# Swapping the halves of the S5 state with copies on ScalarE, and S5 chunk kernels in column quarters

## The chip, the cores and the metric

One core of a Trainium2 chip runs the whole program. The metric is the time of one execution in microseconds (us) on the device; everything is fp32 at the borders. The engines are named as in the profile: PE is TensorE (PEld its weight loads), DVE is VectorE, ACT is ScalarE, POOL is GpSimd, and SP is SyncE, which issues the DMAs.

## The reference

Two blocks run one after the other on 512 tokens of width 1024. The second block (two layers of convolution, neighbourhood attention and feed-forward) isn't touched. The first block mixes the tokens, behind 16 meta tokens, with two state-space branches, SSD and S5, and an MLP follows. The change lies in the S5 branch:

```
bu_re = einsum('blgh,gph->blgp', u, bb_re)      # bb = coef * b, 64 groups g of 16 features h, 64 states p
bu_im = einsum('blgh,gph->blgp', u, bb_im)
# associative scan over the tokens l of s[l] = a * s[l-1] + bu[l], a complex, |a| = exp(lr * step)
_, _, s_re, s_im = lax.associative_scan(combine, (a_re, a_im, bu_re, bu_im), axis=1)
y = einsum('blgp,ghp->blgh', s_re, c_re) - einsum('blgp,ghp->blgh', s_im, c_im) + u * d_skip
y = gelu(y, approximate=False)
v = y @ w_glu + b_glu
y = v[..., :D_S5] * sigmoid(v[..., D_S5:])
```

## The kernel before

**The stages.** `in_proj` makes S5's input u in a layout of chunks of 8 tokens (66 chunks, so 528 columns for the 8 groups of a feature tile). Then the string `ORDER` names the steps of the S5 stage one by one: `P` is `s5_prepare(m)` (the matrices of feature tile m, m from 0 to 7), `S` is `s5_scan(m)`, `x` and `z` are tiles of the input projections for the SSD branch (`xbc_proj`, `z_proj`), `d` and `e` belong to the SSD decays and `r` is `s5_result` (gelu and a split in two parts of one tile). Behind it come `glu`, mixed with the SSD chunks, and the rest. The scans lie between 70 and 276.6 us of the execution.

**Preparing a tile.** `s5_prepare(m)` builds, for the 8 groups of a tile, X (L804 to L806; turned by the `XT` transposes into P, L812), Y (L825), and the kernel within a chunk: eight products `Kp` of 16 rows (L833), four into each of two PSUM tiles, which ACT copies to K (L835, 16x512). DVE adds the skip term to K, and eight DMAs lay it out as the block matrix M (L846).

**Scanning a tile.** The states of the chunks lie with their real parts on partitions 0 to 63 and their imaginary ones on 64 to 127. `s5_scan(m)` makes tables of cosines `cs` and sines `sn` of the chunks' rotations (`sincos`, L781 to L784), makes the chunk states with 2x4 products `S` (L870) and copies each half to SBUF on ACT (L872). To rotate them, each half is multiplied by the constant matrix `perm`, which swaps the two sets of partitions and turns the sign of one (`Sp`, L874); DVE multiplies the result by `sn` (L875), S by `cs` (L876), and adds (L877). Then `tensor_tensor_scan` runs the recurrence over the chunks with the magnitudes `mag8` (L879 copies them to f, L882 is the scan), and the result Z is rotated back in the same way with two more products with `perm` (`Zp`, L885 to L888). Sixteen products `y` (L891 with M, L893 with the states) give the output, which ACT copies to `ye` (L896); SP writes it to DRAM (`yD`, L897). `s5_result` reads it back as `yt` (L903), and ACT makes gelu (L905) and the high part `y5..h` (L909), which `glu` multiplies by its weights.

**Weights.** `W` (L234 to L242) loads a block of weights (`raw`, on SP), ACT casts its high part `whi` (L240) and DVE subtracts it from the block to get the low part `wlo` (L242). `mm3` (L248 to L250) makes three products of each pair of tiles. There are two buffers for `raw` and three for each of the parts.

**What sets the order.** Each engine runs its instructions in one order, which the tile framework's scheduler makes at build time from the program order and from priorities: loads and splits of weights come ahead (`high_priority`), and PE's products of the steps `x` and `z` are laid between the products of a scan. There is one queue for each engine; an instruction that waits holds back all behind it. PSUM has four tiles for the projections (`gps`) and four for all else (`mps`); small tables lie in pools of 16 (`s2`) and 8 (`b4`) buffers.

The matrix, from `constants`:

```
for m in range(64):
    c[m + 64, 256 + m] = 1.0
    c[m, 256 + 64 + m] = -1.0
```

## Time and profile before

| | |
|---|---|
| runs | 2776.68, 2771.53, 2775.11 us; median 2775.11 |
| span of the profiled execution | 2775.2 us (no time around the span is shown for it) |
| PE busy | 2717.2 us, 98% |
| DVE busy | 2020.9 us, 73% |
| ACT busy | 1161.1 us, 42% |
| mean granted clock of TensorE | 0.994 |

The span runs from the first instruction to the last. A share is an average over stages with different limits; the rows of the section on the trace are from the S5 stage and from what follows it directly. In rows of the timeline and of groups, "x2" is a number of records: a float32 product of PE leaves two records, and its start to the next start is the time that it takes in the stream. A bracket at the end of a row tells how long the engine was idle before it and what ended that.

### The profile page before, as it was taken

How to read it: one execution, taken by the hardware profiler on the slowest of the kernel's cores; microseconds unless marked ns; L12 is line 12 of the kernel's file. 1: busy time of each engine (PE TensorE's matmuls, PEld its weight loads, DVE VectorE, ACT ScalarE, POOL GpSimd, SP SyncE). 2: the span in 40 equal slices, each digit the busy share in tenths (PEclk: the TensorE clock that was granted, in tenths of full speed). 3: DMA queues.
4: the chain of work that ended last, by engine and by line, in shares of the span. 5: the costliest groups of instructions: out<-in, count | busy, mean ns of one | idle time of the engine just before them, and what ended most of it. 6: DMA issues, size and time to landing. Idle time of an engine off the chain costs nothing.

```text
span 2775.2 us, 40532 instructions
## 1 busy us (share of the span) xinstructions
PE 2717.2 (98%) x15512; PEld 2340.6 (84%) x15512; DVE 2020.9 (73%) x3969; ACT 1161.1 (42%) x1945; POOL 6.0 (0%) x52
## 2 busy tenths in 40 slices
PE   8999899999999999999999999999999999999998
PEld 8888678788988998878888888888887888988887
DVE  7987678898875575897669888644759966655546
ACT  4443653433444453444454232323553453533333
POOL 0000000000000000000000000000000000000000
PEclk9999999999999999999999999999999999999999
DMA  6223444465432345222324446221342223232332
GB/s 213 68 78 90 115 134 161 159 202 186 132 110 86 121 142 177 95 77 83 101 93 135 155 144 220 96 61 61 105 142 88 86 67 88 91 99 90 103 97 76
DMA packets 157394, 321.08 MB, mean 116 GB/s; under 512 B 39760, under 2 KB 60688, under 8 KB 157200
## 3 DMA queue, kind: packets, MB, share of 16 engines
q1 hardware_dynamic: 157200, 318.49, 36.6%
q8 instruction: 122, 2.00, 0.3%
q14 instruction: 72, 0.59, 0.1%
HBM read 306.53 MB, written 9.54 MB: 114 GB/s over the span
## 4 chain that ended last, share of the span: by engine, by line
PE 80%; DVE 11%; DMA 4%; ACT 3%; issue 2%; SPq 0%; DVEq 0%; ACTq 0%; POOL 0%
PE lat1fu L248 3%; PE lat1fu L249 3%; PE lat1fu L250 3%; DVE wlo L242 3%; PE lat0fu L249 3%; PE lat0fu L248 3%; PE lat0fu L250 3%; PE up L248 2%; PE up L249 2%; PE up L250 2%; PE dn L248 2%; PE dn L249 2%; PE dn L250 2%; PE lat0d L249 1%; PE lat0d L250 1%
## 5 line engine op out<-in xcount | busy, mean ns | idle before, releaser
L240 ACT CAST whi<-raw 128x1024 fp32r<-128x1024 f32 (+3 forms) x486 | 456.8, 940 | 864.7 <-PE ctx0d L249 113.8
L242 DVE TENSOR_TENSOR wlo<-raw,whi 128x1024 fp32r<-128x1024 f32 (+3 forms) x486 | 527.2, 1085 | 204.0 <-ACT whi L240 199.3
L249 PE MATMUL ctx0fu<-ctx0fx,whi 128*128 128x256 f32 x352 | 99.7, 283 | 0.0
L250 PE MATMUL ctx0fu<-ctx0fx,wlo 128*128 128x256 f32 x352 | 99.6, 283 | 0.0
L248 PE MATMUL ctx0fu<-ctx0fx,whi 128*128 128x256 f32 x352 | 99.5, 283 | 0.0
L1134 DVE SCALAR_TENSOR_TENSOR lat1cv<-lat1u,vect,lat1cv 128x512 f32<-128x512 f32 x120 | 86.2, 750 | 0.6
L1134 DVE SCALAR_TENSOR_TENSOR lat0cv<-lat0u,vect,lat0cv 128x512 f32<-128x512 f32 x120 | 86.1, 746 | 0.6
L1453 DVE SCALAR_TENSOR_TENSOR lat0fc<-lat0fu,vect,lat0fc 128x511 f32<-128x511 f32 x44 | 32.9, 749 | 62.7 <-ACT lat0fc L1452 62.7
L248 PEld LDWEIGHTS ctx0fu<-ctx0fx,whi 128*128 128x128 f32 x352 | 67.4, 191 | 1.6
L249 PEld LDWEIGHTS ctx0fu<-ctx0fx,whi 128*128 128x128 f32 x352 | 67.4, 191 | 1.6
L250 PEld LDWEIGHTS ctx0fu<-ctx0fx,wlo 128*128 128x128 f32 x352 | 67.4, 191 | 0.0
L1452 ACT ACTIVATE lat0fc<-lat0fu,vect 128x512 f32<-128x512 f32 x44 | 34.2, 778 | 74.1 <-PE lat0fu L250 74.1
L1493 DVE SCALAR_TENSOR_TENSOR hT<-lat1d,mod1lat,hT 128x512 f32<-128x512 f32 (+1 forms) x40 | 25.5, 644 | 48.2 <-PE lat1d L250 48.0
L1134 DVE SCALAR_TENSOR_TENSOR cxcv<-cxu,vect,cxcv 128x256 f32<-128x256 f32 x120 | 52.3, 485 | 0.7
L250 PE MATMUL ctx0d<-ctx0fh,wlo 128*128 128x256 f32 x176 | 49.9, 285 | 0.3 <-DVE wlo L242 0.3
L248 PE MATMUL ctx0d<-ctx0fh,whi 128*128 128x256 f32 x176 | 49.5, 282 | 0.4 <-ACT whi L240 0.4
L249 PE MATMUL ctx0d<-ctx0fh,whi 128*128 128x256 f32 x176 | 49.8, 284 | 0.0
L985 DVE TENSOR_TENSOR hT<-hT,dn 128x512 f32<-128x512 f32 x40 | 27.5, 687 | 23.1 <-PE dn L250 23.1
L978 DVE SCALAR_TENSOR_TENSOR r<-up,rsbm 128x512 f32<-128x512 f32 x32 | 22.1, 691 | 30.2 <-PE up L250 29.9
L1493 DVE SCALAR_TENSOR_TENSOR hT<-lat0d,mod0lat,hT 128x512 f32<-128x512 f32 x32 | 23.9, 748 | 20.7 <-PE lat0d L250 20.6
L250 PE MATMUL cxg<-cxn1x,wlo 128*128 128x256 f32 x128 | 37.4, 292 | 0.6 <-DVE wlo L242 0.6
L249 PE MATMUL cxg<-cxn1x,whi 128*128 128x256 f32 x128 | 37.5, 293 | 0.0
(3025 smaller groups left out, 9140.4 us busy)
## 6 DMA issues: line engine op xcount, KB each, us to landing
raw<-in_p_in SPq DMA_DIRECT2D x100, 512.0 KB, 3.7
aw<-in_ada SPq DMA_DIRECT2D x192, 256.0 KB, 3.1
raw<-in_p_up SPq DMA_DIRECT2D x88, 512.0 KB, 3.7
raw<-in_p_dn SPq DMA_DIRECT2D x48, 384.0 KB, 3.1
raw<-in_w_up SPq DMA_DIRECT2D x32, 512.0 KB, 3.7
raw<-in_p_cn SPq DMA_DIRECT2D x48, 256.0 KB, 2.6
raw<-in_w_down SPq DMA_DIRECT2D x24, 384.0 KB, 3.0
raw<-in_p_out SPq DMA_DIRECT2D x18, 512.0 KB, 3.8
```

The lines of the kernel that those rows point to most:

```text
L240: nc.scalar.copy(hi, raw)
L242: nc.vector.tensor_sub(lo, raw, hi.bitcast(F32))
L248: mm(ps, w[0], x[0], start=first, stop=False)
L249: mm(ps, w[0], x[1], start=False, stop=False)
L250: mm(ps, w[1], x[0], start=False, stop=last)
L978: V.scalar_tensor_tensor(r, ps, 0.0, rsb, op0=ALU.max, op1=ALU.mult)
L985: V.tensor_add(h[f], h[f], ps)
L1134: V.scalar_tensor_tensor(ac, u[:, k:k + n], self.vec(f"cdw{l}", 4 * k + i), ac, op0=ALU.mult, op1=ALU.add)
L1452: A.activation(u, ps[:, :n], AF.Identity, scale=wv(1), bias=self.vec(f"fdwb{l}", t))
L1453: V.scalar_tensor_tensor(u[:, 1:], ps[:, :n - 1], wv(0), u[:, 1:], op0=ALU.mult, op1=ALU.add)
L1493: V.scalar_tensor_tensor(x, ps, self.mod[l, kind][:, 40 + f:41 + f], x, op0=ALU.mult, op1=ALU.add)
```

## The change

In `s5_scan` the four products with `perm` go, and with them the matrix. ACT copies the chunk states out of PSUM in four pieces of 64 partitions, each to the other half (S then holds the swapped states), and DVE takes the states that aren't swapped from PSUM (`R = ps * cs`). The sign is put into the sine: `sincos` gets a scale for each partition, `turn` = -2 pi sgn. After the scan ACT copies Z in two pieces of 64x528 to the other half, into f, and DVE makes two products of 528 columns where it made four of 264. In `s5_prepare` the four `Kp` products of a half go to PSUM partitions 0, 32, 64 and 96 of one tile (so to four quarters of the array's columns), the halves side by side; ACT copies each quarter with both halves, four copies of 16x2x128. The constants shrink from 588 columns to 460. Removed comments shift the lines.

```diff
@@ -75,9 +75,9 @@
 ROWV = {"dt_bias": (0, 16), "a_log": (16, 16), "d_ssd": (32, 16), "log_step": (48, 64),
         "lam_re": (112, 64), "lam_im": (176, 64)}
 NROW = 240
-CST = {"ident": (0, 128), "tri": (128, 128), "perm": (256, 128), "ones": (384, 128),
-       "cidx": (512, 66), "sgn": (578, 1), "kidx": (579, 9)}
-NCST = 588
+CST = {"ident": (0, 128), "tri": (128, 128), "ones": (256, 128),
+       "cidx": (384, 66), "sgn": (450, 1), "kidx": (451, 9)}
+NCST = 460
 
 
 def constants():
...
@@ -725,6 +722,8 @@
         t = self.b4("pt", 576).rearrange("p (g k) -> p g k", k=9)
         V.tensor_tensor(f, r.unsqueeze(2).to_broadcast([P, 64, 9]),
                         self.C("kidx").unsqueeze(1).to_broadcast([P, 64, 9]), op=ALU.mult)
+        self.turn = self.bp.tile([P, 1], F32, name="turn")
+        V.tensor_scalar(self.turn, self.C("sgn"), -TWO_PI, None, op0=ALU.mult)
         self.r8 = self.bp.tile([P, 64], F32, name="r8")
         self.mag8 = self.bp.tile([P, 64], F32, name="mag8")
         A.copy(self.mag8.unsqueeze(2), pm[:, :, 8:9])
...
@@ -773,18 +772,19 @@
         for t in self.M5:
             nc.gpsimd.memset(t, 0.0)
 
-    def sincos(self, f, t, sn, cs):
+    def sincos(self, f, t, sn, cs, scale=TWO_PI):
         V, A = self.nc.vector, self.nc.scalar
         V.tensor_scalar(t, f, MAGIC, MAGIC, op0=ALU.add, op1=ALU.subtract)
         V.tensor_sub(f, f, t)
         A.activation(cs, f, AF.Sin, scale=TWO_PI / 2)
-        A.activation(sn, f, AF.Sin, scale=TWO_PI)
+        A.activation(sn, f, AF.Sin, scale=scale)
         A.activation(cs, cs, AF.Square)
         V.tensor_scalar(cs, cs, -2.0, 1.0, op0=ALU.mult, op1=ALU.add)
 
     def s5_prepare(self, m):
         nc = self.nc
         V, A, T = nc.vector, nc.scalar, nc.tensor
         gs = slice(8 * m, 8 * m + 8)
...
@@ -824,15 +824,17 @@
             V.tensor_tensor(y4(Y2), g4(self.Gi), c4(C2), op=ALU.mult)
             V.tensor_sub(Yq, Yq, Y2)
         Yg = Y.rearrange("p (g n) -> p g n", g=8)
         Kt = self.b4(f"K{m}", 1024).rearrange("p (g n) -> p g n", g=8)
+        ps = self.mps(f"Kp{m}")
         for q in range(2):
-            ps = self.mps(f"Kp{m}_{q}")
             for r in range(4):
                 g = 4 * q + r
-                T.matmul(ps[:16, r * P:(r + 1) * P], B1[:, g * 16:(g + 1) * 16], Yg[:, g, 0:P],
-                         start=True, stop=True)
-            A.copy(Kt[:16, 4 * q:4 * q + 4].rearrange("p g n -> p (g n)"), ps[:16])
+                T.matmul(ps[32 * r:32 * r + 16, q * P:(q + 1) * P], B1[:, g * 16:(g + 1) * 16],
+                         Yg[:, g, 0:P], start=True, stop=True)
+        Kq = Kt.rearrange("p (q r) n -> p r q n", r=4)
+        for r in range(4):
+            A.copy(Kq[:16, r], ps[32 * r:32 * r + 16, :2 * P].rearrange("p (q n) -> p q n", q=2))
         dI = self.s2(f"dI{m}", P)[:16]
         with self.tc.high_priority(offset=100):
             nc.sync.dma_start(dI, self.I["d5"][:, m * P:(m + 1) * P])
...
@@ -847,21 +849,22 @@
         return Pm, Yg, M
 
     def s5_scan(self, m, mats):
         nc = self.nc
         V, A, T = nc.vector, nc.scalar, nc.tensor
         gs = slice(8 * m, 8 * m + 8)
         Pm, Yg, M = mats
         f, t = self.s2(f"f{m}"), self.s2(f"t{m}")
         sn, cs = self.s2(f"sn{m}"), self.s2(f"cs{m}")
         v3 = lambda x: x.rearrange("p (g c) -> p g c", c=NCH)
         V.tensor_tensor(v3(f), self.r8[:, gs].unsqueeze(2).to_broadcast([P, 8, NCH]),
                         self.C("cidx").unsqueeze(1).to_broadcast([P, 8, NCH]), op=ALU.mult)
-        self.sincos(f, t, sn, cs)
+        self.sincos(f, t, sn, cs, self.turn)
         U = self.hT[S5U[m]]
         S, R = self.s2(f"S{m}"), t
+        halves = ((slice(0, 64), slice(64, P)), (slice(64, P), slice(0, 64)))
         hf = [slice(0, HALF), slice(HALF, TOK)]
         for q in range(2):
             ps = self.mps(f"S{m}_{q}")
...
@@ -869,22 +872,20 @@
                 g = 4 * q + r
                 T.matmul(ps[:, r * NCH:(r + 1) * NCH], Pm[:, g * P:(g + 1) * P],
                          U[:, g * NCH:(g + 1) * NCH], start=True, stop=True)
-            A.copy(S[:, hf[q]], ps[:, :HALF])
-            pp = self.mps(f"Sp{m}_{q}")
-            T.matmul(pp[:, :HALF], self.C("perm"), S[:, hf[q]], start=True, stop=True)
-            V.tensor_mul(f[:, hf[q]], pp[:, :HALF], sn[:, hf[q]])
-            V.tensor_mul(R[:, hf[q]], S[:, hf[q]], cs[:, hf[q]])
+            for a, b in halves:
+                A.copy(S[a, hf[q]], ps[b, :HALF])
+            V.tensor_mul(R[:, hf[q]], ps[:, :HALF], cs[:, hf[q]])
+            V.tensor_mul(f[:, hf[q]], S[:, hf[q]], sn[:, hf[q]])
         V.tensor_add(R, R, f)
         m8 = f
         A.copy(v3(m8), self.mag8[:, gs].unsqueeze(2).to_broadcast([P, 8, NCH]))
         nc.gpsimd.memset(v3(m8)[:, :, 0:1], 0.0)
         Z = S
         V.tensor_tensor_scan(Z, m8, R, 0.0, op0=ALU.mult, op1=ALU.add)
-        for q in range(2):
-            pp = self.mps(f"Zp{m}_{q}")
-            T.matmul(pp[:, :HALF], self.C("perm"), Z[:, hf[q]], start=True, stop=True)
-            V.tensor_mul(f[:, hf[q]], pp[:, :HALF], sn[:, hf[q]])
-            V.tensor_mul(R[:, hf[q]], Z[:, hf[q]], cs[:, hf[q]])
+        for a, b in halves:
+            A.copy(f[a], Z[b])
+        V.tensor_mul(R, Z, cs)
+        V.tensor_mul(f, f, sn)
         V.tensor_sub(R, R, f)
         py = self.mps(f"y5{m}")
         for g in range(8):
```

Where this moves instructions is read from the order in which each engine's instructions stand. PE at the scan of tile 2 before: the second K group (`Kp`), the state products with a `perm` product behind each half (`S`, `Sp`), the swap of the scan's result (`Zp`), and the first `y`; the `xbc` rows are the filler.

```order
L249 MATMUL xbc_0_2205<-xg0l,whi_2201 128x264
L833 MATMUL Kp_1_1435<-Y_1419,bc_1395 16x128 x4
L870 MATMUL S_0_1465<-hT_85,P_1151 128x66 x4
L250 MATMUL xbc_0_2139<-xg0h,wlo_2137 128x264
L250 MATMUL xbc_1_2140<-xg0h,wlo_2137 128x264
...
L249 MATMUL xbc_0_2139<-xg2l,whi_2135 128x264
L874 MATMUL Sp_0_1471<-S_1464,cst 128x264
L870 MATMUL S_1_1475<-hT_85,P_1151 128x66 x4
...
L885 MATMUL Zp_0_1489<-S_1464,cst 128x264
L885 MATMUL Zp_1_1493<-S_1464,cst 128x264
L891 MATMUL y_1498<-hT_85,M_0_640 128x64
L250 MATMUL xbc_0_2139<-xg7h,wlo_2137 128x264
```

PE at the same place after: the K groups lie around both halves of S, and what follows the second one is 74 `xbc` products and then the `y` products.

```order
L833 MATMUL Kp_1422<-Y_1412,bc_1388 16x128 x4
L873 MATMUL S_0_1459<-hT_85,P_1149 128x66 x4
L873 MATMUL S_1_1468<-hT_85,P_1149 128x66 x4
L892 MATMUL y_1486<-hT_85,M_0_642 128x64
...
L833 MATMUL Kp_1422<-Y_1412,bc_1388 16x128 x4
L247 MATMUL xbc_0_2112<-xg0h,wlo_2110 128x264
...
L245 MATMUL xbc_0_2178<-xg5h,whi_2174 128x264
L246 MATMUL xbc_0_2178<-xg5l,whi_2174 128x264
L894 MATMUL y_1486<-t_1448,Y_1162 128x64
L892 MATMUL y_1486<-hT_85,M_0_642 128x64
```

Both halves' `Sp` and the two `Zp` are gone, the first `y` has moved ahead of the second K group, and no product that waits for the scan stands between the K group and the second `y`.

ACT at the same scan before: the copies of K, the tables, the copies of S, a weight cast, the magnitudes.

```order
L835 COPY K_1428<-Kp_0_1429 16x512
L835 COPY K_1428<-Kp_1_1435 16x512
L781 ACTIVATE cs_1456<-f_1453 128x528
L782 ACTIVATE sn_1455<-f_1453 128x528
L783 ACTIVATE cs_1456<-cs_1456 128x528
L872 COPY S_1464<-S_0_1465 128x264
L872 COPY S_1464<-S_1_1475 128x264
L240 CAST whi_2390<-raw_2388 128x1024
L879 COPY f_1453<-mag_578 128x528
```

And after, with the two copies of Z at the end:

```order
L837 COPY K_1421<-Kp_1422 16x2x128 x4
L781 ACTIVATE cs_1450<-f_1447 128x528
L782 ACTIVATE sn_1449<-f_1447,turn 128x528
L783 ACTIVATE cs_1450<-cs_1450 128x528
L876 COPY S_1458<-S_0_1459 64x264 x2
L876 COPY S_1458<-S_1_1468 64x264 x2
L237 CAST whi_2358<-raw_2356 128x1024
L881 COPY f_1447<-mag_580 128x528
L886 COPY f_1447<-S_1458 64x528 x2
```

The order of the kinds is kept; the K copies, now all four behind both K groups, stand ahead of the cosine as before, and two copies of Z have come in behind the magnitudes.

ACT at the end of the stretch (tile 7) before, up to the copy of the output; the four `z` are activations of the last z tiles:

```order
L872 COPY S_2711<-S_0_2712 128x264
L872 COPY S_2711<-S_1_2722 128x264
L240 CAST whi_3262<-raw_3260 128x1024
L879 COPY f_2700<-mag_578 128x528
L240 CAST whi_3295<-raw_3293 128x1024
L589 ACTIVATE z_2779<-z_0_3068,rs1k 128x256
L589 ACTIVATE z_2780<-z_0_3068,rs1k 128x256
L589 ACTIVATE z_2781<-z_1_3069,rs1k 128x256
L589 ACTIVATE z_2782<-z_1_3069,rs1k 128x256
L240 CAST whi_3445<-raw_3443 128x1024
L896 COPY ye_2762<-y_2745 128x512
```

And after:

```order
L876 COPY S_2679<-S_0_2680 64x264 x2
L876 COPY S_2679<-S_1_2689 64x264 x2
L586 ACTIVATE z_2741<-z_0_3030,rs1k 128x256
L586 ACTIVATE z_2742<-z_0_3030,rs1k 128x256
L237 CAST whi_3224<-raw_3222 128x1024
L881 COPY f_2668<-mag_580 128x528
L586 ACTIVATE z_2743<-z_1_3031,rs1k 128x256
L586 ACTIVATE z_2744<-z_1_3031,rs1k 128x256
L237 CAST whi_3257<-raw_3255 128x1024
L886 COPY f_2668<-S_2679 64x528 x2
L237 CAST whi_3407<-raw_3405 128x1024
L897 COPY ye_2724<-y_2707 128x512
```

Two `z` activations now stand ahead of the copy of the magnitudes, and all four and two weight casts ahead of the copies of Z.

SP at the end of the stretch before, where `raw` are glu's weights:

```order
L234 DMA raw_3260<-in_w_glu 128x1024
L234 DMA raw_3293<-in_w_glu 128x1024
L695 DMA hT_86<-in_xT 128x512
L234 DMA raw_3443<-in_w_glu 128x1024
L234 DMA raw_3476<-in_w_glu 128x1024
L695 DMA hT_88<-in_xT 128x512
L897 DMA yD_210<-ye_2762 128x512
L903 DMA yt_2765<-yD_203 128x8x64
```

And after:

```order
L231 DMA raw_3222<-in_w_glu 128x1024
L231 DMA raw_3255<-in_w_glu 128x1024
L692 DMA hT_86<-in_xT 128x512
L231 DMA raw_3405<-in_w_glu 128x1024
L231 DMA raw_3438<-in_w_glu 128x1024
L231 DMA raw_3472<-in_w_glu 128x1024
L904 DMA yt_2727<-yD_203 128x8x64
L898 DMA yD_210<-ye_2724 128x512
```

A further `raw` load has come ahead of the write of tile 7's output, the one `hT` load has moved behind, and the first `yt` load has passed the write of `yD`.

## Rows read from the trace of the kernel before

**Rows 1.** The page, part 1: busy us (share of the span) xinstructions.
```profile
PE 2717.2 (98%) x15512; PEld 2340.6 (84%) x15512; DVE 2020.9 (73%) x3969; ACT 1161.1 (42%) x1945; POOL 6.0 (0%) x52
```

**Rows 2.** Windows: stretch, length, busy PE PEld DVE ACT POOL (records), clock, DMA share, GB/s.
```profile
70.00:276.60 206.60, 198.20 (x1556) 184.13 (x1554) 176.04 (x303) 85.01 (x144) 1.91 (x18) 1.00 0.28 78
```

**Rows 3.** PE's waits to 300 us: us in total, times, longest us.
```profile
PE glug L248 <- ACT y50h L909: 8.0, 1, 8.0
...
PE Zp L885 <- DVE S L882: 3.6, 8, 0.7
...
PE xbc L248 <- ACT whi L240: 2.3, 3, 1.5
...
PE Sp L874 <- ACT S L872: 0.6, 3, 0.2
```

**Rows 4.** Lines: ns min/median/max, first and last start us, forms.
```profile
L872 ACT COPY S<-S x16: 349/375/382, 89.6 to 269.0; 128x264 f32<-128x264 f32 x16
...
L782 ACT ACTIVATE sn<-f x8: 627/628/639, 88.0 to 264.8; 128x528 f32<-128x528 f32 x8
...
L879 ACT COPY f<-mag x8: 632/633/640, 94.9 to 271.4; 128x528 f32<-128x528 f32 x8
```

**Rows 5.** Timeline of the scan of tile 2: start us, us, engine line op.
```profile
146.13 0.28 PE L250 MATMUL xbc<-xg2h,wlo 128*128 128x264 f32 x1
...
146.35 0.71 PE L874 MATMUL Sp<-S,cst 128*128 128x264 f32 x2
...
147.02 0.28 PE L249 MATMUL xbc<-xg3l,whi 128*128 128x264 f32 x1
...
148.20 1.22 DVE L242 TENSOR_TENSOR wlo<-raw,whi 128x1024 fp32r<-128x1024 f32 x1
...
149.33 1.25 DVE L882 TENSOR_TENSOR_SCAN S<-f,t 128x528 f32<-128x528 f32 x1
...
149.95 0.28 PE L249 MATMUL xbc<-xg7l,whi 128*128 128x264 f32 x1
...
150.73 1.13 PE L885 MATMUL Zp<-S,cst 128*128 128x264 f32 x4 [0.50 <-DVE S L882]
...
151.69 0.33 PE L891 MATMUL y<-hT,M 128*128 128x64 f32 x2
...
152.59 0.70 DVE L888 TENSOR_TENSOR t<-t,f 128x528 f32<-128x528 f32 x1
```

**Rows 6.** Chain that ended last, 105 to 170 us: start us, us, what.
```profile
165.30 1.85 PE Kp L833 x16
```

**Rows 7.** Timeline of the end of the stretch: start us, us, engine line op.
```profile
276.61 0.84 ACT L589 ACTIVATE z<-z,rs1k 128x256 f32<-128x256 f32 x2 [2.90 <-PE z L250]
...
276.89 0.43 PE L893 MATMUL y<-t,Y 128*128 128x64 f32 x2 [0.32 <-DVE t L888]
...
281.10 1.28 ACT L905 ACT_TABLE_LOAD   x1
...
281.47 8.79 SPq L903 DMA_DIRECT2D yt<-yD  x8
...
286.05 0.63 ACT L905 ACTIVATE yt<-yt 128x512 f32<-128x512 f32 x1 [3.67 <-DMA yt<-yD]
...
288.80 0.80 PE L248 MATMUL glug<-y50h,whi 128*128 128x512 f32 x1 [7.99 <-ACT y50h L909]
...
290.62 1.28 ACT L497 ACT_TABLE_LOAD   x1
...
291.92 0.27 ACT L497 ACTIVATE sp<-sp 128x80 f32<-128x80 f32 x1
```

**Rows 8.** Windows of one us behind the stretch, columns as in rows 2.
```profile
283.00:284.00 1.00, 0.00 (x0) 0.00 (x0) 0.00 (x0) 0.00 (x0) 0.00 (x0) 0.50 0.74 165
...
292.00:293.00 1.00, 1.00 (x4) 0.81 (x3) 0.75 (x2) 1.00 (x2) 0.00 (x0) 0.50 1.43 228
...
295.00:296.00 1.00, 1.00 (x7) 0.79 (x6) 0.90 (x4) 1.00 (x3) 0.00 (x0) 1.00 0.00 0
```

11 lines of the change are left out of this document (4 added, 7 removed).

## The prediction

> **What bounds the kernel now.** I first asked which engine fills the stretch in which the changed lines work, then what that engine waits for, then how long the chain behind the wait is. The S5 scans lie between 70 and 276.6 us. There PE is busy for 198.20 of 206.60 us and DVE for 176.04, at a granted clock of 1.00 [rows 2]; over the whole span PE is busy for 98% [rows 1]. So the stretch ends when PE has done its products, and a product taken off PE shortens it, as long as no new wait takes its place. DVE, the next in line, has 176 us of work and allows at most some 30 us of gain. PE's waits are small: 3.6 us in eight waits of the Z swap (Zp) for the scan, 0.6 us in waits of the S swap (Sp), and some for weights; the one large wait, 8.0 us, is that of the first glu product behind the stretch [rows 3].
>
> The base: the profiled execution has a span of 2775.2 us, and nothing of its time is shown around the span; that is 0.1 above the median of the runs, 2775.11. Sums are made from 2775.2. About 0.2%, or 5.5 us, is what a measurement of this kernel can tell from no change: under 2769.6 is faster, over 2780.7 slower.
>
> **Part 1, the swap products go.** Price of one Sp in the stream: between an xbc product at 146.13 and another at 147.02 stand one Sp (two records) and one xbc product, 0.89 us [rows 5]. The 24 xbc products from 147.02 to 149.95 follow each other every 0.122 us [rows 5], so Sp takes 0.89 - 2x0.12 = 0.65 us. A pair of Zp runs from 150.73 to the y product at 151.69, 0.96 us [rows 5]. Sixteen Sp and eight pairs of Zp: 10.4 + 7.7 = 18.1 us, all on PE. PE's waits in front of them, 3.6 + 0.6 = 4.2 us [rows 3], go with them. Together 22.3.
>
> **Part 2, the K products in four column quarters.** Sixteen records, eight products, take 1.85 us in the stream [rows 6], 0.23 each; the 64 of all tiles take 14.8 us. After the change four neighbours write four quarters. No row of before has two products side by side in one array. Bounds: nothing gained if they stay in sequence; three quarters of 14.8 = 11.1 us if four run at once; below nothing I exclude, since the same records are issued as before. I take half, 5.6 us: each product is two records on the same quarter, issued one behind the other, so that only the second record of one and the first of the next can overlap freely.
>
> The Trainium skill ("TensorE: Matmul & The Clock Gate", "Why this matters for your kernels") reports 2.38 times for three column tiles of 512 columns. By that page, as an estimate, the products would take 6.2 us and the gain would be 8.6; no run shown here can confirm it.
>
> **Part 3, the chain behind the K products gets longer.** PE is fed by a chain that starts at the second K group of a scan: ACT copies K, makes the cosine and the sine, copies S; DVE multiplies, adds and scans; the result goes to y. The order of the instructions is kept in this: the K copies stand ahead of the sines on ACT, so S waits on ACT although its products are done. Before, PE met the chain at Sp, at Zp and at y, with xbc or z products (fillers) between them. After, it meets it once: all fillers stand ahead of the 15 last y products, and PE waits there for the whole rest.
>
> Length after, from rows: four K copies at 0.35 (the S copy of 264 columns took 0.375 [rows 4], and a K copy now has 256), three activations at 0.63 [rows 4], four S copies at 0.35, by durations 4.7 us; neighbours overlap a little, so 4.2. Then the last product 0.4 (half of a 528-wide operation, 0.70 [rows 5]), the sum 0.7, a weight difference 1.22 that stands in front of the scan [rows 5], the scan 1.25 [rows 5], two swap copies of Z at 0.63 (as the 528-wide copy of the magnitudes [rows 4]), a product 0.7, the difference 0.7: 6.2 us, and five hand-overs of 0.15. In all 11.2 us from the second K group to y.
>
> Cover: the number of products between them, read from the order, by 0.121 (xbc) or 0.118 us (z). Tile by tile, chain minus cover:
> tile 0: 14 - 12.0 = 2.0 (DVE is full there); tiles 1, 2 and 4: 11.2 - 8.9 = 2.2 to 2.3 (74 products); tile 3: 12.6 (two more convolution steps on DVE) - 6.7 (57) = 5.9; tile 5: 11.7 - 6.1 (52) = 5.6; tile 6: 11.9 - 11.1 = 0.8. Sum 21.0; in tiles 3 and 5 part of it is spent earlier on, waiting for weights, but it is the same time. About 2 of it are weight waits that PE has already [rows 3], so 19 are new. Tile 7 is the end, below. Bounds: each of the chain's copies may be 0.15 us shorter or longer, 8 copies, seven tiles, some 8 us either way: 10 to 27 for the new waits.
>
> What else is in the same instructions: DVE does one 528-wide product where it did two 264-wide ones; its total falls by 1 to 2 us, and is not what ends the stretch. What is queued behind the new waits on ACT are weight copies (whi) and convolution steps; PE has weights for one tile ahead, so that I cost this at nothing beyond the 19; if that cover is gone, it is one weight difference of 1.22 us [rows 5] per scan. The smaller constant block is loaded before the stretch, and nothing waits for it: nothing.
>
> **Part 4, the end of the stretch.** After tile 7 the last z product is followed by y at 276.89 (a wait of 0.32), the table load for gelu at 281.10, eight loads of yt from 281.47, the first gelu at 286.05, and glu at 288.80 after 7.99 us of waiting [rows 7]. After the change two z activations (0.84 us the pair [rows 7]) and a weight cast stand ahead of the copies of Z on ACT, so y waits for some 4.5 us and not 0.3. That does not add to the 8 us: the loads of yt that carry the first glu input don't need tile 7, and glu waits for them. What moves glu is the place of those loads on SP: in the new order they stand behind the fifth raw load, which waits for a buffer that a weight difference on DVE frees, and that stands behind the last tile's difference. I get some 1.2 us later, and 0.8 for two more table loads on ACT that are partly hidden. So -2.0; bounds 0 (the wait as long as before) and -7.1 (4.5 of waiting on y, two loads of 1.28 [rows 7]).
>
> A table load takes 1.28 us, and the next activation begins 1.30 after it began, at 291.92 after 290.62 [rows 7]. The Trainium skill ("ScalarE: Activation LUTs", "What ACT_TABLE_LOAD costs") gives 1283 ns for the load, which the trace shows too, and 1380 ns for a drain besides, 2.66 us for a switch. Two switches would cost 5.3 by the page and 2.6 by the row; the row decides.
>
> **The sum.** 22.3 + 5.6 - 19 - 2.0 = 6.9 us. Two of the new waits, in tiles 3 and 5, are the longest in the stretch, and the clock may fall there once: an allowance of half a fall, 1.0 (price below). 2775.2 - 5.9 = 2769.3 us.
>
> **Rivals.**
> *The chain is shorter, or the quarters all run at once.* If all four quarters overlap, 5.5 us more are gained: 2764. If besides each of six chains is 1.5 us shorter (the copies of S overlap as the two engines' pieces can), 9 more: 2755. For it: ACT is busy for only 85 of 206.6 us [rows 2]. Against it: copies on ACT are strictly in a row, and each half's copies need the bank whole.
> *The columns do nothing.* The change doesn't do what it says if the four products of a group stay in sequence; the 5.6 are missing: 2775, no change. For it: each is a group of two dependent records on one quarter. Against it: only an absence of rows.
> *Slower: the clock.* The stretch runs at 1.00 with PE waiting for 1.5 us at most [rows 2, 3]; around the wait of 8 us it is at 0.50 (1.2 of 2.4 GHz), and is still there at 292 to 293, where PE does 4 products of 512 columns in the microsecond that later holds 7 [rows 8]. From 288.8 to 293 that cost 4.2 x (1 - 4/7) = 1.8 us, say 2. If each of the seven new waits lets the clock fall, that is 14 us: 2768.3 + 14 = 2782. It decides at waits of some 2.2 us, four of the seven; if those leave the clock at 1.00, two waits alone cost at most 4.
>
> **How the numbers follow.** Forecast, 2764 to 2774: 0.46, a little over half of it below 2769.6. Shorter chain or full overlap, about 2755 to 2764: 0.20. No overlap, 2775: 0.18. Clock, 2782: 0.16. Faster by over 0.2%: 0.27 + 0.20 = 0.47. Within: 0.19 of the forecast, 0.16 of the third, 0.02 of the clock = 0.37. Slower: 0.16. The time is that of the likeliest, 2769. Range for 8 in 10: 2757, as part of the second case lies below, to 2782, as part of the clock case lies above.
>
> **What would show it.** No Sp or Zp rows, and PE busy less by 18 plus what the quarters give. Right on part 2: the 16 records of a tile's K products in some 1.2 us and not 1.85. Right on part 3: before the second y product of tiles 1, 2 and 4 a wait on DVE's difference of 2 to 2.5 us, and with the weight waits 5 to 6 in tiles 3 and 5, the clock at 1.00. Right on part 4: glu begins some 1 to 2 us later after the last z product than the 12.2 us of before (288.80 - 276.6). Wrong if the waits on y sum up to under 10 or over 27 us, if the clock row shows 0.50 inside the stretch, or if glu's start moves by more than 4.

## The result, and the profile after

The changed kernel takes 2799.84 us in the median of its runs (2797.63 to 2806.55); the kernel before takes 2775.89 beside it. The ratio is 1.009, with an interval of 1.0075 to 1.0104: some 24 us slower, where 2769 had been forecast and 2782 was the upper end. The profiled execution has a span of 2804.8 us, 29.6 more than before. A profile shows one single execution, which can lie off the median of its kernel: here it is the slowest of four, 6.7 us above the median, and those of e2, e4 and e13 below lie 10.7, 4.5 and 6.7 above theirs.

The page, part 1, as in [rows 1]:

```profile
PE 2727.9 (97%) x15448; PEld 2351.0 (84%) x15448; DVE 2019.9 (72%) x3954; ACT 1185.7 (42%) x1995; POOL 5.9 (0%) x52
```

PE has 64 records fewer, and 28 us less to do, as will be seen, and yet is busy for 10.7 us *more* than in [rows 1]. Its products must have become longer somewhere. The window of the scans tells where (columns as in [rows 2]; the last z product ends at 295.9 now, where it ended at 276.6):

```profile
70.00:295.90 225.90, 200.10 (x1505) 186.50 (x1503) 173.07 (x287) 105.59 (x191) 1.92 (x18) 0.86 0.25 69
```

It is 19.3 us longer, and its granted clock is 0.86 where [rows 2] has 1.00. PE is idle for 25.8 us of it (225.90 - 200.10) where it was idle for 8.4. PE's waits up to 320 us, as in [rows 3]:

```profile
PE y L894 <- DVE t L889: 10.6, 5, 4.7
PE z L246 <- DVE wlo L239: 7.5, 2, 3.7
...
PE xbc L245 <- ACT whi L237: 4.3, 3, 2.6
PE XT L812 <- DVE X L806: 3.3, 4, 1.2
PE glug L245 <- ACT y50h L910: 3.1, 1, 3.1
```

Zp and Sp are gone, and with them their waits. In their place PE waits for the difference t ahead of y, for weights (wlo, whi) and for X. What such a wait does is seen at the first scan, in windows of one us (columns as in [rows 2]) and in PE's timeline (start us, us, engine line op, wait):

```profile
102.00:103.00 1.00, 0.00 (x0) 0.00 (x0) 1.00 (x3) 0.30 (x1) 0.00 (x0) 1.00 0.00 0
103.00:104.00 1.00, 0.00 (x0) 0.00 (x0) 1.00 (x2) 0.00 (x0) 0.00 (x0) 0.78 0.00 0
104.00:105.00 1.00, 0.74 (x4) 0.74 (x4) 1.00 (x3) 0.08 (x1) 0.00 (x0) 0.50 0.00 0
...
127.00:128.00 1.00, 1.00 (x9) 1.00 (x8) 0.71 (x2) 0.97 (x3) 0.00 (x0) 0.77 0.41 66
128.00:129.00 1.00, 1.00 (x11) 1.00 (x10) 0.65 (x3) 0.95 (x4) 0.00 (x0) 1.00 0.52 73
```

```profile
104.26 0.69 PE L894 MATMUL y<-t,Y 128*128 128x64 f32 x2 [3.71 <-DVE t L889]
104.74 0.64 PE L892 MATMUL y<-hT,M 128*128 128x64 f32 x2
105.17 0.63 PE L894 MATMUL y<-t,Y 128*128 128x64 f32 x2
```

PE waits 3.71 us; toward the end of the wait the clock goes from 1.00 to 0.50 (1.2 of 2.4 GHz), and it comes back only at 127 to 128, 24 us later. In between PE is busy for most of the time, and idle three more times, for 0.5, 0.8 and 2.6 us. There are eight stretches at half clock between 60 and 350 us, 4 to 25 us long; before there was one, behind the wait of 8 us [rows 8].

So that runs can be compared, I use two sums from here on. **Idle** is the time in which PE does nothing between 60 and 330 us (for the changed kernel 60 to 350, as its scans end later). **Clock loss** is the sum over one-us windows of PE's busy time times (1 - granted clock): what the same products would have saved at the full clock. Before: idle 17.4, clock loss 2.2. After: idle 36.6, clock loss 34.8. The account of the 29.6 us then closes to within 2 us: 28.3 of work gone from PE (18.1 of swap products and 10.2 of K), 19.2 more idle, 32.6 more clock loss, and in the rest of the program 0.3 less idle and 8.0 more clock loss (1.7 of it ahead of 60 us): -28.3 + 19.2 + 32.6 - 0.3 + 8.0 = 31.2.

The K products ran in their quarters. One group of eight products (PE's timeline, before and after; 16 records took 1.85 us in [rows 6]):

```profile
84.15 1.05 PE L833 MATMUL Kp<-Y,bc 128*16 128x128 f32 x8
...
87.78 0.41 PE L833 MATMUL Kp<-Y,bc 128*16 128x128 f32 x8
```

And the copies that the change puts on ACT (lines: ns min/median/max, first and last start us, forms; those replaced are in [rows 4]):

```profile
L837 ACT COPY K<-Kp x32: 358/366/368, 79.1 to 270.4; 16x256 f32<-16x256 f32 x32
L876 ACT COPY S<-S x32: 371/375/378, 94.3 to 291.8; 64x264 f32<-64x264 f32 x32
L886 ACT COPY f<-S x16: 630/632/634, 100.4 to 298.3; 64x528 f32<-64x528 f32 x16
```

A copy of half of the partitions takes as long as one of all: 375 ns, as in [rows 4].

### The profile page after: what moved, and what is told of

The parts are those of the page before. It is cut to its first block, busy times and chain, and to the rows that moved or that the text cites. A ratio compares the mean times of both kernels' runs of the same rounds, so it can differ in the third digit from the quotient of the medians.

```text
span 2804.8 us, 40442 instructions
## 1 busy us (share of the span) xinstructions
PE 2727.9 (97%) x15448; PEld 2351.0 (84%) x15448; DVE 2019.9 (72%) x3954; ACT 1185.7 (42%) x1995; POOL 5.9 (0%) x52
## 4 chain that ended last, share of the span: by engine, by line
PE 80%; DVE 11%; ACT 4%; DMA 3%; issue 2%; SPq 0%; DVEq 0%; ACTq 0%; POOL 0%
PE lat1fu L245 3%; PE lat1fu L247 3%; PE lat1fu L246 3%; DVE wlo L239 3%; PE lat0fu L246 3%; PE lat0fu L245 3%; PE lat0fu L247 3%; PE up L246 2%; PE up L245 2%; PE up L247 2%; PE dn L245 2%; PE dn L246 2%; PE dn L247 2%; PE lat0d L246 1%; PE lat0d L247 1%
## 5 line engine op out<-in xcount | busy, mean ns | idle before, releaser
L894 PE MATMUL y<-t,Y 128*128 128x64 f32 x128 | 30.2, 325 | 10.6 <-DVE t L889 10.6
L1494 DVE SCALAR_TENSOR_TENSOR hT<-lat0d,mod0lat,hT 128x512 f32<-128x512 f32 x32 | 23.9, 748 | 21.2 <-PE lat0d L247 21.1
```

The costliest lines, as they stand in the source:

```text
L894: T.matmul(py[:, g * 64:(g + 1) * 64], Yg[:, g, 16:144], R[:, g * NCH + 1:g * NCH + 65], start=False, stop=True)
L1494: V.scalar_tensor_tensor(x, ps, self.mod[l, kind][:, 40 + f:41 + f], x, op0=ALU.mult, op1=ALU.add)
```

## The experiments

The theories at the start. **A:** the copies of the state on ACT make PE wait, and the waits lower the clock. **B:** the quarters do, by themselves. **C:** the waits alone, at their own length, are the loss. **D:** DVE stands at the addition to K (L844) until ACT's four copies are there, and everything behind it comes late. Ratios are against the kernel before, run on the same chip.

### The parts alone

e1 is the kernel before with only the quarters, e2 with only the swaps, e4 with the quarters and the S swap, Z still swapped by products.

```diff
 e1:
...
-            A.copy(Kt[:16, 4 * q:4 * q + 4].rearrange("p g n -> p (g n)"), ps[:16])
+                T.matmul(ps[32 * r:32 * r + 16, q * P:(q + 1) * P], B1[:, g * 16:(g + 1) * 16],
+                         Yg[:, g, 0:P], start=True, stop=True)
...
+        for r in range(4):
+            A.copy(Kq[:16, r], ps[32 * r:32 * r + 16, :2 * P].rearrange("p (q n) -> p q n", q=2))
```

> The kernel before with only the K products in column quarters (one PSUM tile, four copies behind both groups); the swap products with perm stay. Theory A, the waits: PE's new waits on the scan's result let its clock fall, and they come from the copies between partitions; here there are none, so the clock stays at 1.00 from 70 to 276 us, and the K products give what they save, about 1 us a tile: 2768 us. Theory B, the quarters: products on a quarter of the columns count as little work and let the clock fall: clock under 0.95 in the stretch, 2785 us or more. Theory C, the idle time alone (the waits cost what they last, the clock little): 2768 as in A.

> The changed kernel with the K products as before (all at position 0, two copies); the swaps of the state's halves are copies on ScalarE. Theory A: the waits of 2 to 5 us on the scan's result are there, the clock falls as in the changed kernel, and the 8 us of the K products are missing: 2800 to 2808 us. Theory B: without quarters the clock stays at 1.00, and the swap products' 22 us less 19 us of waits leave about 2775.

> Half of the change: K in quarters and the swap of S by copies on ScalarE; the swap of Z stays two products with an unsigned perm, behind the scan. Theory A: the products of Z break PE's wait in two and keep it under 2 us, so the clock mostly stays at 1.00; 8 us from K and 10 us from Sp come in, 4 to 8 us of waits go out: 2762 to 2768. Theory B: clock under 0.95, 2785 or more. Theory C: about 2765 with any clock.

Measured: e1 2793.4 us, ratio 1.0062 (1.0045 to 1.008), idle 32.1, clock loss 10.4. e2 2779.3, 1.0015 (1.0002 to 1.0028), idle 25.9, clock loss 18.9. e4 2796.7, 1.0066 (1.0049 to 1.0083), idle 41.0, clock loss 22.8. The quarters alone take 10.2 us of work from PE and cost 16 us. (The sums of e2 are of an execution of 2790.0 us.) By time alone these three lie nearer to theory B, which had 2785 or more with the quarters and about 2775 without, than to A. The traces show what happens. e1's waits of PE from 60 to 330 us:

```profile
PE XT L812 <- DVE X L806: 8.7, 4, 6.3
...
PE Sp L876 <- ACT S L874: 7.7, 5, 2.2
```

and where the 6.3 come from, on DVE (timeline):

```profile
108.73 2.37 DVE L562 SCALAR_TENSOR_TENSOR xbcT<-xr,vect,xbcT 128x528 f32<-128x528 f32 x3 [3.02 <-ACT xbcT L559]
111.02 0.69 DVE L804 TENSOR_TENSOR X<-s5Ar,bc 128x512 f32<-128x512 f32 x1
```

The third tile's X starts at 111.02; before it started at 103.03:

```profile
103.03 0.69 DVE L804 TENSOR_TENSOR X<-s5Ar,bc 128x512 f32<-128x512 f32 x1
```

In e1's order one convolution tile more (three steps of L562) stands ahead of it on DVE, and the last steps wait 3.02 us for ACT. Nothing in the edit asks for this: the scheduler has put the instructions in another order. PE waits 6.3 us for this X, and the clock then is at half from 110 to 124. So the fall follows a wait, which theory B does not need, and a new theory comes up, **E: the order.** That the quarters do nothing to the clock by themselves is not shown yet.

### The addition on GpSimd

Theory D, tried by taking the addition off DVE: e5 from the changed kernel, e6 from e1, e7 from the kernel before.

```diff
-        V.tensor_add(Kt[:16, :, 0:16], Kt[:16, :, 0:16], d3)
+        nc.gpsimd.tensor_add(Kt[:16, :, 0:16], Kt[:16, :, 0:16], d3)
```

> The changed kernel with one instruction a tile moved: the addition of the skip term to K (16x128) runs on GpSimd, not on VectorE. Theory D, VectorE's queue: in the changed kernel VectorE stood 23.5 us at that addition until the four copies of K on ScalarE were done (11.8 before), and all its work behind it stood too. Without it PE's waits shrink and the clock falls less often: 2768 to 2785 us. Theory A, the waits that come from ScalarE's copies of the state: nothing in their chain is shorter, 2792 us or more.

> The quarters alone, the swaps by perm as before, and the addition to K on GpSimd. Theory D: the loss of the quarters alone (16 us in the first experiment) was VectorE's longer wait at that addition and PE's waits that follow from it; now the 10 us that the K products save come through: 2758 to 2770 us. Theory A: the copies of K stand ahead of the copies of S on ScalarE all the same, 2785 or more.

> The kernel before with the addition to K on GpSimd and nothing else. Theory D: VectorE's 11.8 us of waits at the addition go; PE is the bound there, and gains only what of its waits hung on them, 3 to 10 us: 2767 to 2774. Theory A: 2777, no change.

Measured: e5 2814.6 us, 1.0129 (1.0106 to 1.0151), clock loss 46.5; e6 2798.4, 1.0065 (1.0044 to 1.0086); e7 2789.7, 1.0039 (1.0024 to 1.0054). All three miss what D had for them: e5 is slower than the changed kernel, e6 no faster than e1. DVE's largest waits from 60 to 330 us, in the changed kernel and in e5, show why:

```profile
DVE K L844 <- ACT K L837: 23.5, 8, 6.5
DVE cs L784 <- ACT cs L783: 7.5, 4, 6.7
```

```profile
DVE cs L784 <- ACT cs L783: 29.4, 6, 7.4
```

With the addition gone from DVE, DVE stands at the next thing that it needs from ACT, the cosine, which ACT makes right behind the same four copies: 31.0 us at both places in the changed kernel, 29.4 in e5. So the addition is not the place that matters; that DVE loses time to the copies of K is not disproved by this. And e7 moves one 16-partition addition off a busy engine in the kernel before, and costs 10 us, more than either theory had: again an order that came out otherwise (PE waits 6.3 us for X at the same place as in e1).

### Unread products, first try

e3 and e8 add four and two products of Z per scan to the changed kernel, which nobody reads.

```diff
+            pj = self.mps(f"Zj{m}_{q}")
+            for _ in range(2):        # e8: 1
+                T.matmul(pj[:, :HALF], self.C("ident"), Z[:, hf[q]], start=True, stop=True)
```

> The changed kernel plus four products of 128x264 float32 a scan that read the scan's result Z and that nobody reads: PE works in the last part of its wait for y, as it did on Zp before, and the chain of ScalarE and VectorE is as long as in the changed kernel. Theory A: the clock stays at 1.00 in most of the stretch, and of the 33 us that the low clock took at least 20 come back: 2768 to 2780 us, faster than the changed kernel although it does more. Theory C: PE's work is not what decides, the chain is: 2800 us or above. Theory B: 2800, the quarters are still there.

> As the third experiment, with two unread products of Z a scan in place of four, so about 8 us of PE work less. Theory A: two products, as before the change, are enough to keep the clock at 1.00 in most of the stretch: clock loss stays near 11 us and 8 us of work go: 2786 to 2790. If the clock needs the longer filling, it falls again as in the changed kernel: 2797 or more.

Measured: e3 2796.0 us, 1.0064 (1.0049 to 1.0079), clock loss 10.7; e8 2799.7, 1.0077 (1.0059 to 1.0095), clock loss 24.2. e3 does some 15 us more work than the changed kernel and yet takes no more time, at a third of its clock loss, with the quarters in place. That speaks against B and C, which both had 2800 or above. It is no hit for A either, which had 2768 to 2780: the clock loss fell by the 20 us and more that A asked for, but the added products took most of it. In e8 two products a scan were not enough to keep the clock up, as its second alternative had it (2797 or more). And the order had changed here as well, so the clock's price can't be read from these two.

### The order held

From here on the order is taken out of the question: a table holds each engine to the order in which the kernel before issues its instructions.

```diff
+def pin(tc):
+    ins = list(tc.nc.cur_bb.bb.instructions)
+    info = mybir.DependencyInfo(mybir.DependencyClass.NoSync, mybir.DependencyReason.DATA)
...
+            if prev is not None:
+                tc.add_manual_dep(ins[at], ins[prev].name, info, reason="issue_after")
+            prev = at
```

e9 is e1 in before's order, e10 the whole change, e12 the swaps alone. e11 is the opposite: before's operations, with DVE and ACT in e1's order.

> The kernel before with the column quarters alone, as in e1_quarters, but every engine is held to the order in which the kernel before issues its instructions (order edges without a wait for completion; the four copies of K stand where the second of the two copies stood). What differs from e1_quarters is the order alone, what differs from the kernel before is the quarters alone. If the order is what made e1_quarters slow: 2764 to 2772 us (16 product groups at 0.64 us less are 10.2 us, of which the waits give some back), idle time of PE from 60 to 330 us under 24 us, clock loss there under 5 us. If the operations are (the copies of K that start only when both groups are done, or PE that runs out of work sooner): 2785 us or more in this order too, with waits of PE for X or S over 6 us and a clock loss of 8 us or more.

> The whole change, every engine held to the order of the kernel before: the copies of S stand where the single copy stood, the two copies of Z stand on ScalarE where the scan ends in the trace of before, the products on VectorE take the places of those they replace. If the order is the cause: 2750 to 2768 us (28 us less work of PE, minus waits of the size of before's), no stretch at half clock that before does not have beyond one. If the operations are the cause (the copies lengthen the chain from S to y, or PE is relieved of so much that it waits for VectorE): 2785 us or more, with waits of PE for t ahead of y over 6 us, and a clock loss of 20 us or more.

> The kernel before with none of the change's operations, but VectorE and ScalarE held to the order in which e1_quarters issues (33 rows of VectorE and about 18 of ScalarE stand elsewhere; PE's order is the scheduler's and comes out near e1_quarters' too). If the order is the cause: 2785 us or more, with a wait of PE for the third tile's X of about 6 us near 105 us and half clock behind it. If the operations are: 2774 to 2781 us, clock loss from 60 to 330 us under 4 us.

> The swaps by ScalarE alone (K's products and copies as before), every engine held to the order of the kernel before; the third corner of the square with e9_quarters_order and e10_change_order. If what the operations cost in that order is the shortened work of PE that turns into waits, and each wait into a stretch at half clock: 2780 to 2790 us, waits of PE for t ahead of y of 5 us or more, a clock loss of 8 us or more from 60 to 330 us. If the swaps' shorter chain pays in a good order, and only the quarters do harm: 2765 to 2775 us, periods of the scans under those of before.

Measured: e9 2786.2 us, 1.003 (1.0019 to 1.0042); e10 2794.0, 1.0053 (1.004 to 1.0066); e11 2786.8, 1.0027 (1.0016 to 1.0038); e12 2799.6, 1.0074 (1.0062 to 1.0086). Order alone costs 8 us (e11: no operation changed), and it does so in the way of e1: PE waits as long for the third tile's X (PE's timeline), and the clock is at half behind it, from 111 to 122.

```profile
114.57 1.11 PE L812 MATMUL XT<-cst,X 128*128 128x128 f32 x4 [6.29 <-DVE X L806]
```

But the quarters in the old order cost 8 as well (e9), and the whole change 16 (e10). Neither theory is right by itself: going back to the old order gives e1 8 of its 16 us back, and the changed kernel 8 of its 24. The swaps alone do worse in the old order than in the scheduler's own (e2), and worse than the 2780 to 2790 that was the slower of e12's two alternatives, so the old order is no ideal either. The table itself costs nothing that shows in e15 below, which is before with one operation less and held in the same way: ratio 0.9997.

e9 shows what goes wrong beside the order, near 90 us. PE's timeline, and windows of five us (columns as in [rows 2]):

```profile
90.32 0.51 PE L250 MATMUL xbc<-xg0h,wlo 128*128 128x264 f32 x2 [2.94 <-DVE wlo L242]
```

```profile
85.00:90.00 5.00, 2.38 (x20) 2.17 (x19) 4.56 (x9) 3.32 (x8) 0.10 (x1) 1.00 0.21 32
90.00:95.00 5.00, 4.68 (x21) 4.40 (x22) 3.15 (x7) 2.21 (x5) 0.00 (x0) 0.63 0.38 84
95.00:100.00 5.00, 5.00 (x29) 4.79 (x29) 4.12 (x7) 1.21 (x2) 0.21 (x2) 0.69 0.00 0
```

Before, the clock stayed at 1.00:

```profile
89.29 0.51 PE L250 MATMUL xbc<-xg0h,wlo 128*128 128x264 f32 x2 [1.41 <-DVE wlo L242]
```

```profile
85.00:90.00 5.00, 3.59 (x29) 3.26 (x27) 4.97 (x10) 3.12 (x7) 0.10 (x1) 1.00 0.30 43
```

DVE has hardly a gap ahead of this place in both. The wait has grown by 1.5 us. A later load of bc ahead of the first X shifts both engines by 0.6 us, and is not the edit's: in kernels with the same program up to there that load is waited for from 0.3 us (before) to 1.5 (e15). Counted from it, PE, with shorter K products, is there 1.1 us sooner, and wlo comes 0.4 later, which DVE spends on waiting for the four copies of K.

The other kernels in this order make a test of this place. Those without the quarters wait there as before does, 1.41 us (e12, e14, e15), whatever their load of bc; those with the quarters wait 2.92 to 2.94 (e9, e10, e13, e16, e17). Behind the longer wait the clock falls to half at 91 to 95, in all five; behind the shorter it stays at 1.00, in all four. And e18, which has the quarters and unread products in this wait (below), keeps 1.00 there. The same product in e12, e10 and e18:

```profile
91.63 0.52 PE L247 MATMUL xbc<-xg0h,wlo 128*128 128x264 f32 x2 [1.41 <-DVE wlo L239]
...
92.26 0.51 PE L247 MATMUL xbc<-xg0h,wlo 128*128 128x264 f32 x2 [2.94 <-DVE wlo L239]
...
91.12 0.51 PE L254 MATMUL xbc<-xg0h,wlo 128*128 128x264 f32 x2 [0.34 <-DVE wlo L246]
```

So here the wait brings the clock down, and not the quarters as such.

With the clock at half, e9 is 3.5 us late at the end of the first scan (its copy ye starts at 107.7, before at 104.2). From that copy to the last one it takes 179.7 us, before 176.3: in seven intervals with up to 1.3 us less PE work each, none is shorter by more than 0.2 us, and the whole is longer. PE's other new wait is for the copies of S, 5.5 us in four (0.6 in three in [rows 3]); ACT has four copies of K ahead of them, where it had two.

### The waits filled

If the clock is what a wait costs, then products that do nothing must make the kernel faster, in the same order. e13 is e10 with four unread products in y's bank just ahead of y's own; e18 has 75 of them where e13 still waited, 19 of these ahead of the glu.

```diff
 e13:
+        for _ in range(4):
+            T.matmul(py[:, 0:256], M[:, 7, :], U[:, 0:256], start=True, stop=True)
 e18:
+    FEED = {"xbc11": 6, "xbc1": 3, "z2": 3, "glug0": 19, "y50": 4, "y51": 6, "y52": 4, "y53": 4,
+            "y54": 7, "y55": 4, "y56": 9, "y57": 6}
+        for _ in range(self.FEED.get(name, 0)):
+            self.nc.tensor.matmul(ps[:, :256], self.C("ident"), self.cst[:, 128:384],
+                                  start=True, stop=True)
```

> As e10_change_order, order and all, with four products more per scan that nobody reads (128 rows by 256 columns from M and U, into y's bank just before y's own products overwrite it): some 2 us of work for PE in front of the place where it waited for t, 6 of 8 times and 13.8 us in all. It does strictly more than e10_change_order in the same order. If the waits cost mainly by the clock that falls after them: clock loss from 60 to 330 us under 15 us (24.5 in e10_change_order), and the time the same or up to 10 us less, 2782 to 2794 us. If the clock falls for another reason, or a wait costs no more than its length: the products that outlast the waits come on top, 2795 to 2806 us.

> As e13_change_order_fed (the whole change in the order of the kernel before, with unread products in front of y's), the unread products now set by what waits were left there: 128 rows by 256 columns, 0.43 us each, 4 to 9 in y's bank, 6 ahead of the tile of xbc that waited 2.9 us for wlo at 92 us, 3 ahead of two more, and 19 ahead of the first product of the glu, which waited 8.4 us; 75 in all, 32 us of work, none read. If the waits cost by the clock that falls after them: clock loss from 60 to 330 us under 10 us (19 in e13), the glu's wait under 1 us and no half clock behind it, time 2768 to 2780 us. If the clock falls for another reason than PE's waits: clock loss 15 us or more, 2784 us or more.

Measured: e13 2783.7 us, 1.0018 (1.0008 to 1.0028). e18 2776.2, 0.9995 (0.9986 to 1.0004). So 14 us of useless work (32 products of 0.43) made e10 10 us faster, and 32 us of it (75) made it 16 (by the ratios) to 18 us faster (by the medians). e13's time is within what was expected if the waits cost by the clock, 2782 to 2794; its clock loss, 19.1 us in the profiled execution, is above the 15 that went with it. The waits for t in e10, and in e13:

```profile
PE y L894 <- DVE t L889: 13.8, 6, 3.8
```

```profile
PE y L896 <- DVE t L889: 5.4, 4, 2.1
```

The window from 60 to 330 us, before, e10 and e18 (columns as in [rows 2]):

```profile
60.00:330.00 270.00, 252.59 (x1856) 228.03 (x1855) 215.69 (x367) 124.93 (x210) 1.91 (x18) 0.98 0.33 93
```

```profile
60.00:330.00 270.00, 232.32 (x1716) 214.48 (x1715) 202.58 (x338) 135.91 (x234) 1.91 (x18) 0.89 0.32 85
```

```profile
60.00:330.00 270.00, 259.61 (x1918) 235.31 (x1918) 210.26 (x347) 144.94 (x255) 1.91 (x18) 0.97 0.33 91
```

In e18 PE is busy for 259.61 us of the 270, does more products, and the clock is 0.97 and not 0.89. That shows the price: in e10 the 28.3 us taken from PE came back as 20.3 us of idle time *and* 22.3 of clock loss, and when the idle time is filled most of the clock loss goes with it. With the waits filled the change is even with the kernel before, no better. e18's expectation held: clock loss 6.7 us, the glu no longer among PE's larger waits. The quarters are in it too, so that theory B is out.

The account for the pinned kernels, us, against the profiled execution of before (work: PE's time at the full clock, an unread product 0.43):

| | work | idle | clock loss | sum | span, measured |
|---|---|---|---|---|---|
| e9 quarters | -10.2 | +9.0 | +8.1 | +6.9 | +8.4 |
| e12 swaps | -18.1 | +13.0 | +29.3 | +24.2 | +23.7 |
| e10 whole change | -28.3 | +20.3 | +22.3 | +14.3 | +18.0 |
| e13 whole change, fed | -14.5 | +10.7 | +16.9 | +13.1 | +13.1 |
| e18 fed more | +4.0 | -7.0 | +4.5 | +1.5 | +1.9 |

### Why the saved work turns into waits

e14 makes the chain from S to the scan longer in the kernel before; e15 to e17 make the chain behind the scan shorter, in before, in e9 and in e10, by leaving out the difference R - f behind the scan, so that a part of the computation is missing from them.

```diff
 e14:
+        for _ in range(2):
+            V.tensor_mul(R, S, cs)
         V.tensor_add(R, R, f)
 e15 to e17:
-        V.tensor_sub(R, R, f)
         py = self.mps(f"y5{m}")
```

> The kernel before in its own order, with two more 128x528 multiplications per scan on VectorE that write again what is there (R = S cs), between the products with the table and the sum ahead of the scan: some 1.3 us per tile on VectorE and in the chain from S to y, 10 us in all, nothing else changed. If VectorE and its chain set the pace of the scans: 2788 us or more, 10 us at least plus what the clock adds. If PE sets it and the chain has slack: 2778 to 2783 us.

> The kernel before in its own order without the subtraction R = R - f behind the scan: y's products take R as it is (a part of the computation is left out). The chain from the scan to y is some 1.5 us shorter per tile, VectorE has 0.7 us less per tile, PE the same work. If the chain of VectorE alone sets the pace: 2767 us or less (1.5 us on 7 intervals). If PE and the chain are about even, so that neither gains without the other: 2772 to 2779 us.

> The quarters in the order of the kernel before, as e9_quarters_order, and the subtraction behind the scan left out as in e15 (a part of the computation is left out). If PE and the chain are about even, relief of both together pays what relief of PE alone (e9, 2786 us) did not: 2764 to 2774 us. If what made e9 slow is something else (the copies of K on ScalarE): 2780 us or more.

> The whole change in the order of the kernel before, as e10_change_order, and the subtraction behind the scan left out (a part of the computation is left out): y's products wait for R alone, not for the copies of Z on ScalarE and the multiplication with them, some 2.5 us per tile. If the chain was what turned the 28 us of saved PE work into waits: 2755 to 2772 us, waits of PE for t ahead of y under 4 us in all (13.8 in e10), clock loss under 10 us. If not: 2782 us or more.

Measured: e14 2801.5 us, 1.0077 (1.0065 to 1.009). e15 2777.8, 0.9997 (0.9987 to 1.0008). e16 2784.0, 1.0026 (1.0016 to 1.0035). e17 2775.6, 0.9998 (0.9987 to 1.0008). PE's waits in e14 for the scan (3.6 us in [rows 3]), and in e17 for t (13.8 in e10):

```profile
PE Zp L887 <- DVE S L884: 13.8, 8, 2.0
```

```profile
PE y L893 <- DVE t L887: 3.7, 3, 1.8
```

e14: 1.3 us more per scan ahead of the scan shows up almost whole in PE's waits, and costs 23 us, double the 10.4 that were added. So in the kernel before the scan is ready just when PE comes to it. e15: behind the scan the kernel before has slack, and nothing is gained there. e17 against e10: with that chain shorter the changed kernel gains 18.4 us, as its waits for t go from 13.8 to 3.7 (by the ratios it gains 15). The same cut gains nothing in e15 and 2 us in e16, so it isn't the 0.7 us a tile that DVE is spared. So it was this chain that turned a good part of the saved work into waits in e10; but even with it cut short, e17 is only even with before (idle +10.3, clock loss +21.1, work -28.3), above the 2755 to 2772 and the clock loss of under 10 that were expected if the chain were all. e16 gave 2784, and all its runs are over 2780, so that "PE and this chain are about even" (2764 to 2774) is not what made e9 slow; the quarters' waits are for wlo and for the copies of S (5.5 us), not for what lies behind the scan.

Did the change shorten the chain? From the end of a tile's S products to the end of the difference, in the median of the eight tiles: 8.1 us before, 8.5 in e10 and in e12. (In the changed kernel S's products stand ahead of the second K group, and this stretch is 13.1.) The swap products were off PE's account, but the copies that replaced them are no shorter in the chain.

## Why the prediction was wrong, by its own steps

**The swap products and the K products: right in kind, K under-sized.** All Sp and Zp are gone, 18.1 us by the rows. Four neighbours in four quarters take 0.41 us and not 1.05, so 16 groups gain 10.2 us where half of 11.1 had been taken: nearly the whole upper bound. The reason given for the half, that only the second record of one product and the first of the next can overlap freely, is not borne out by these rows. The estimate by the Trainium skill ("TensorE: Matmul & The Clock Gate", "Why this matters for your kernels") had been 8.6; the rows give somewhat more.

**The new waits: the chain was right, the places only in part, and the total by luck.** From the end of the second K group to the end of the difference the chain takes 11.5 us in tiles 1, 2 and 4 of the changed kernel, where 11.2 had been worked out. Tile 2, on PE and on DVE:

```profile
154.31 0.41 PE L833 MATMUL Kp<-Y,bc 128*16 128x128 f32 x8
...
165.50 0.71 DVE L889 TENSOR_TENSOR t<-t,f 128x528 f32<-128x528 f32 x1
```

The sum had 19 us of new waits and 2.0 at the end against 4.2 that went, 16.8 net; the idle time grew by 19.2. But in tiles 1, 2 and 4 PE waits 1.0 us, nothing and 0.4 for y where 2.2 each had been forecast: in tiles 1 and 4 the clock is at half for a part of the filler, which then takes longer, and in tile 2 PE stands 2.3 us for an earlier filler's xr instead. Tile 0 waits 3.7 and not 2.0. In tiles 3 and 5 the wait for weights came as said, 3.7 us each, with 0.7 and nothing on y behind it, where 5.9 and 5.6 stood:

```profile
188.49 0.39 PE L246 MATMUL z<-wlo,xg0h 128*128 128x256 f32 x1 [3.74 <-DVE wlo L239]
```

The waits on y in tiles 0 to 6 sum up to 5.8 us, under the 10 that the prediction gave as a sign that it is wrong; with tile 7 they are 10.6. The rest is whi (4.3), X (3.3), xr and Y, to which the sum gave nothing: "PE has weights for one tile ahead, so that I cost this at nothing beyond the 19" failed for these 4.3 (2.3 before).

**The end of the stretch: near in size by luck, wrong in its path.** glu starts at 310.92, 15.3 us after the last z product's start at 295.58; before it was 12.5. That is 2.8 more, 2.0 had been taken. The wait on y that was forecast, some 4.5 us, came (4.7). But it was said not to count, because glu hangs on the loads of yt, and these were to come late by their place on SP. ACT's timeline after:

```profile
307.26 0.59 ACT L897 COPY ye<-y 128x512 f32<-128x512 f32 x1 [6.22 <-PE y L894]
307.86 1.28 ACT L906 ACT_TABLE_LOAD   x1
309.15 0.63 ACT L906 ACTIVATE yt<-yt 128x512 f32<-128x512 f32 x1
```

The first load of yt had started at 302.70, and ACT does not wait for it, as it did for 3.67 us in [rows 7]. ACT waits for y: the copy of y stands ahead of gelu in ACT's order, PE began y 4.7 us after the z products, and ran it at half clock, in 6.7 us where it had taken 3.6.

**The clock: this step failed.** An allowance of 1.0 us stood in the sum, and the rival had a price of 2 us for each of seven falls. Measured: clock loss 34.8 us where it was 2.2 before, in eight stretches at half clock; these 32.6 us are about what lies between the forecast and the result, as the other terms, work and idle time, came within 5 us of theirs. The price of 2 us, read off the one fall of before, holds for the two cheapest (1.7 each, 4 to 5 us long); the six others cost 3.0 to 9.6 us and are 8 to 25 us long. In the longest, of 24 us, PE met further waits. The mechanism was named as the slower rival, at a chance of 0.16, and was the one that came. The Trainium skill ("TensorE: Matmul & The Clock Gate", "A second HAM failure mode: psum-queue depth-cycling") describes, for another kernel in bf16, PE that idles briefly between groups of products so often that its clock goes back and forth; e10, e13 and e18 agree, with eight, six and three stretches at half clock and losses of 24.5, 19.1 and 6.7 us in the same order.

**The first paragraph: its condition was not met.** "A product taken off PE shortens it, as long as no new wait takes its place": new waits did take it, and nearly whole. e9 takes 10.2 us off in the same order, and not one interval between scans gets shorter by more than 0.2 us. That PE was busy for 96% of the stretch did not make it the bound with room behind it; DVE and the chain to the scan came in at the same time (e14).

**What the prediction did not weigh: the order.** It read the changed order for what stands ahead of what in each scan, and took everything else as kept. e11 shows that the order alone is worth 8 us in the kernel before; between the changed kernel and e10, with the same operations, lie some 8 to 10.

**What stays open.** Why the quarters help beside the swaps (e12 to e10, 5.6 us) and cost 8 alone is not settled beyond the account above; the falls lie at other places in each kernel. And the split into order, chain and clock is not a sum: each makes the others larger.

## What to carry to other kernels

Where an engine is busy for nearly all of a stretch, ask what its waits would be with the work gone, before the work is counted as gain: if a second engine and a chain arrive within 0.7 us of it, as at every Zp here, the saved time can turn into waits. On TensorE such waits cost more than their length here, and the test for it is cheap: put unread products into them, in the same order, and see whether the kernel gets faster. When a scheduler sets the order, run the edit once in the old order too; otherwise the edit and the order are measured as one.

## What the runs showed of the hardware

Idle time of PE came with clock loss beside it: 20.3 us with 22.3 in e10, 9.0 with 8.1 in e9, 13.0 with 29.3 in e12; and 32 us of useless products were worth 16 to 18 us (e18). Half clock followed a wait of 2.92 to 2.94 us in five kernels, where a wait of 1.41 at the same place left the clock at 1.00 in four others. It could last for 24 us in which PE was busy for most of the time and waited three more times, for 0.5 to 2.6 us, as after 104 us in the changed kernel. Products of 16 columns in four column quarters ran at 2.6 times the pace of one column after another (1.05 to 0.41 us for four). And a copy of 64 partitions by ScalarE took 375 ns for 264 columns, the same as one of 128.
